# A feed-forward on TensorE: gate and up from seven products of halves, and a down stage of its own for every 512 tokens

## Chip, cores and metric

The kernel runs on one core of a Trainium2 chip. The metric is the device time of one execution in microseconds (us). Three timed runs of the kernel before lie between 2853.63 and 2855.86 us, median 2854.32.

## What is computed

One decoder layer over 2048 tokens of width 1024, in float32. The first part (an input projection, two mixers over groups of heads, an output projection and the residual) is not touched by the change. The second part is

```python
n = rms_norm(h, rms2_g[l])
h = h + (jax.nn.silu(n @ ffn_gate[l]) * (n @ ffn_up[l])) @ ffn_down[l]
return rms_norm(h, final_g)
```

with `ffn_gate` and `ffn_up` of 1024 x 2816 and `ffn_down` of 2816 x 1024, that is 22 tiles of 128 hidden channels. In the kernel, n has the channels on the partitions, so that `n @ W` is a sum over 8 slices of 128 channels.

Float32 products are made of three TensorE matmuls. Each operand is split into a high part (a cast to fp32r, on ScalarE) and a low part (the rest, a subtraction on VectorE or GpSimd), and high x high, high x low and low x high are summed in PSUM. The code has names that end in `h` and `l` for them.

## The kernel before

**First part.** The instructions are written out in an order that a planner class, `Order`, sets: `streams` lists generators (projection, mixers, output projection and so on), and the planner takes the next piece from the one that is earliest by its own account. A string that a generator yields is an event it waits for. Two generators at the end of the list prepare the second part: `ffn_w` loads the first gate and up weights, and `prep_b` prepares n for the first 1024 tokens while the last jobs of the output projection run. A job is one block of rows of the output projection; `om` events mark that its operands are ready, `op` is its PSUM tile, and its result goes to `hs` in DRAM, by way of the tile `hx`.

**Preparing n.** `prep2` (L966) loads 512 rows of `hs` for two channel slices into `hk`, scales the rows by the reciprocal norm (L977 on ScalarE, L979 on VectorE), transposes them with TensorE into the PSUM tile `tcn` (L985), and ScalarE (L995) and VectorE (L997) write the two parts into SBUF.

**Feed-forward.** `phase_b` runs over two halves of 1024 tokens. For each half all eight row tiles of h, 128x1024 each, stay in SBUF. The loop goes over 11 pairs of channel tiles. `split` loads a weight tile (512 KB) and splits it. `up(f, nb)` makes gate (`gps`) and up (`ups`) for one channel tile and 512 tokens: 8 slices x 3 matmuls for each, L1486 to L1488; then ScalarE takes silu (L1490), VectorE multiplies (L1491), and the result is split into `hh` and `hl`, which stay in SBUF. `down(nb)` multiplies the hidden block with the down weights: for each row tile and each 512 columns 2 channel tiles x 3 matmuls go into a PSUM tile `dn` (L1508 to L1510), which VectorE adds to h (L1511). After the last pair, each row tile is squared and summed on ScalarE (L1513), `row_rs` computes the reciprocal norm in nine small VectorE operations, two VectorE operations scale the row tile (L1520), and it is written out. n for the second half of the tokens is prepared inside the last pair of the first.

The order within this part is that of a scheduler in the framework. SyncE issues all loads and stores, in one queue. Tiles of a tag share a fixed number of buffers; `bt` deals out the tags that `SEQ` lists, in turn, and these are buffers that the first part has used.

Of the kernel before, what the change touches and what calls it, by code (L numbers as in the profile page):

```python
# [11 lines left out]
F32 = mybir.dt.float32  # L12
# [257 lines left out]
class K:  # L270
# [61 lines left out]
    def phase_a(self, ctx):  # L332
# [8 lines left out]
        self.n2, self.nb_ = {}, {}  # L341
# [93 lines left out]
                
# [386 lines left out]
    def out_w(self, nb):  # L822
# [3 lines left out]
        for x in range(3):  # L826
# [18 lines left out]
            for k in range(KT):  # L845
                if not k % 2:
                    if x < 2:
                        yield f"ok{k // 2}" if x else f"zk{b}.{k // 2}"
                        pair = [self.s.tile([128, 2, BLK], F32R, name="wo", tag=t, bufs=4) for t in ("nh", "nl")]
                    else:  # L850
                        pair = [self.bt("W2", "wo", [128, 2, BLK], F32R) for _ in range(2)]
                self.wo[x, k] = h, _ = [t[:, k % 2] for t in pair]
# [80 lines left out]
    def prep_b(self, nb):  # L933

        for n in range(2):
            yield f"rs{n}"
            yield f"b{nb * HP - 1}"
            yield f"a{nb * HP - 1}"
            for kp in range(KT // 2):
                if n:  # L940
                    yield f"wo2.{KT - 1}"
                    if kp == KT // 2 - 1:
                        yield f"mt{len(self.jobs(nb)) - 1}"
                yield from self.prep2(0, n, kp)

    def ffn_w(self, nb):

        nc = self.nc
        x = [j[2] for j in self.jobs(nb)]
        yield f"om{len(x) - 1 - x[::-1].index(1)}"  # L950
        yield f"b{nb * HP - 1}"
        yield f"a{nb * HP - 1}"
        yield f"gm{2 * nb - 1}"
        self.first = []
        for n in ("wg", "wu"):
            raw = self.bt("raw", "raw", [128, 1024])
            nc.sync.dma_start(out=raw, in_=self.I[n][0])
            yield
            hi, lo = [self.bt("W", n + c, [128, 1024], F32R) for c in "hl"]
            nc.scalar.copy(out=hi, in_=raw)  # L960
            yield
            nc.vector.tensor_tensor(out=lo, in0=raw, in1=hi.bitcast(F32), op=ALU.subtract)
            self.first.append((hi, lo))
            yield

    def prep2(self, half, n, kp):  # L966

        nc = self.nc
        r0 = half * 1024 + n * 512
        hb = self.hs[r0:r0 + 512, :].rearrange("(j p) d -> p j d", p=128)  # L970
        x = self.bt("raw", "hk", [128, 4, 256])
        nc.sync.dma_start(out=x, in_=hb[:, :, kp * 256:(kp + 1) * 256])
        yield
        for j in range(4):
            r = self.rsb[:, r0 // 128 + j:r0 // 128 + j + 1]
            if j % 2:
                nc.scalar.activation(out=x[:, j, :], in_=x[:, j, :], func=AF.Copy, scale=r)  # L977
            else:
                nc.vector.tensor_scalar(out=x[:, j, :], in0=x[:, j, :], scalar1=r, scalar2=None, op0=ALU.mult)  # L979
        yield 1000.0  # L980
        for i in range(2):
            k = kp * 2 + i
            ps = self.ma("tcn", [128, 512])
            for j in range(4):
                nc.tensor.transpose(out=ps[:, j * 128:(j + 1) * 128], in_=x[:, j, i * 128:(i + 1) * 128],  # L985
                                    identity=self.ident)
            yield
            if n * KT + k < 1:
                hl = self.bt("n4", "n2", [128, 2, 512], F32R)
                h, l = hl[:, 0], hl[:, 1]  # L990
            else:
                h = self.bt("n2", "n2h", [128, 512], F32R)
                l = self.bt("n2", "n2l", [128, 512], F32R)
            g = self.g2[:, k:k + 1]
            nc.scalar.activation(out=h, in_=ps, func=AF.Copy, scale=g)  # L995
            yield
# [618 lines left out]
```

## Time and profile before

| | |
|---|---|
| median of three timed runs | 2854.32 us |
| the profiled execution | 2848.36 us, of which the span is 2846.5 us |
| TensorE / VectorE / ScalarE / GpSimd busy | 96% / 50% / 35% / 24% |
| first part | until about 1360 us |
| feed-forward | from there to the last matmul at 2836.1 us |
| after the last matmul | 10.4 us |

Shares of busy time are means over both parts. Of the feed-forward alone the rows of the windows below tell: there GpSimd has nothing to do. Durations of single matmuls in the rows overlap, since a matmul starts before the one ahead of it has ended; the distance of their starts is what counts.

### The profile page before, as it was taken

The numbers are of one execution on the slowest core, as the hardware profiler recorded it, in microseconds if no ns is written. First come the engines' busy times: TensorE is split into PE (matmuls) and PEld (weight loads), VectorE is DVE, ScalarE is ACT, GpSimd is POOL, SyncE is SP. The second block draws the span as 40 slices with busy tenths as digits, with TensorE's granted clock in tenths as the row PEclk, the third lists the DMA queues.
The fourth block names the chain that finished last, engine by engine and source line by source line (L and its number), as shares of the span: only waits on it lengthen the run. The fifth ranks groups of instructions, "written<-read, shape, count | busy, mean of one in ns | idle before, by whom it ended". The sixth has DMA issues, their size and how long they took to land.

```text
span 2846.5 us, 38755 instructions
## 1 busy us (share of the span) xinstructions
PE 2719.6 (96%) x14856; PEld 2193.3 (77%) x14856; DVE 1423.0 (50%) x2878; ACT 1009.0 (35%) x1955; POOL 685.3 (24%) x1470
## 2 busy tenths in 40 slices
PE   5999899989999998999999999999999999999998
PEld 4777677777777777777888888888888888888886
DVE  6475766675666566565433333333373333333335
ACT  7455555664455454444211111111151111111112
POOL 3656465646555565310000000000000000000000
PEclk9999999999999999999999999999999999999999
DMA  4112221231121113456411111111161111111111
GB/s 146 56 60 75 90 67 57 71 100 57 60 75 56 57 64 92 158 195 219 148 45 55 49 45 45 45 45 50 49 228 51 48 50 52 45 45 45 45 45 60
DMA packets 123467, 216.56 MB, mean 76 GB/s; under 512 B 10641, under 2 KB 52337, under 8 KB 123281
## 3 DMA queue, kind: packets, MB, share of 16 engines
q1 hardware_dynamic: 123280, 214.08, 23.6%
q8 instruction: 117, 1.92, 0.3%
q14 instruction: 70, 0.57, 0.1%
HBM read 188.87 MB, written 25.17 MB: 75 GB/s over the span
## 4 chain that ended last, share of the span: by engine, by line
PE 54%; DMA 2%; DVE 1%; ACT 0%; issue 0%; SPq 0%; DVEq 0%; POOL 0%; ACTq 0%; POOLq 0%
PE gps L1486 6%; PE gps L1488 6%; PE ups L1488 6%; PE gps L1487 6%; PE ups L1486 6%; PE ups L1487 6%; PE dn L1509 6%; PE dn L1508 6%; PE dn L1510 6%; DMA hk<-hs 1%; DMA hx<-in_x 1%; PE op L901 1%; PE op L902 1%; PE op L903 1%; PE tcn L985 0%
## 5 line engine op out<-in xcount | busy, mean ns | idle before, releaser
L631 PE MATMUL zd<-nh,w_hi 128*128 128x512 f32 x832 | 358.3, 431 | 1.1 <-ACT w_hi L606 0.7
L633 PE MATMUL zd<-nh,w_lo 128*128 128x512 f32 x832 | 332.3, 399 | 6.6 <-POOL w_lo L608 6.6
L1511 DVE TENSOR_TENSOR h<-dn,h 128x512 f32<-128x512 f32 x352 | 242.7, 690 | 180.8 <-PE dn L1510 180.5
L632 PE MATMUL zd<-nl,w_hi 128*128 128x512 f32 x832 | 330.3, 397 | 0.1
L608 POOL TENSOR_TENSOR w_lo<-w_raw,w_hi 128x512 fp32r<-128x512 f32 x208 | 276.9, 1335 | 207.1 <-ACT w_hi L606 170.4
L1509 PE MATMUL dn<-wdl,hh 128*128 128x512 f32 x704 | 278.4, 395 | 0.0
L1508 PE MATMUL dn<-wdh,hh 128*128 128x512 f32 x704 | 277.7, 395 | 0.0
L1510 PE MATMUL dn<-wdh,hl 128*128 128x512 f32 x704 | 277.1, 394 | 0.0
L1488 PE MATMUL gps<-n2h,wgl 128*128 128x512 f32 x660 | 259.9, 394 | 0.0
L1488 PE MATMUL ups<-n2h,wul 128*128 128x512 f32 x660 | 259.9, 394 | 0.0
L1486 PE MATMUL gps<-n2h,wgh 128*128 128x512 f32 x660 | 259.8, 394 | 0.0
L1486 PE MATMUL ups<-n2h,wuh 128*128 128x512 f32 x660 | 259.7, 394 | 0.0
L1487 PE MATMUL gps<-n2l,wgh 128*128 128x512 f32 x660 | 259.6, 393 | 0.0
L1487 PE MATMUL ups<-n2l,wuh 128*128 128x512 f32 x660 | 259.5, 393 | 0.0
L1491 DVE TENSOR_TENSOR sgu<-sgu,ups 128x512 f32<-128x512 f32 x88 | 60.2, 684 | 396.9 <-PE ups L1488 385.8
L1453 ACT CAST wdh<-raw 128x1024 fp32r<-128x1024 f32 x44 | 46.2, 1050 | 466.0 <-PE dn L1510 250.3
L633 PEld LDWEIGHTS zd<-nh,w_lo 128*128 128x128 f32 x832 | 158.8, 191 | 46.2 <-POOL w_lo L608 9.7
L631 PEld LDWEIGHTS zd<-nh,w_hi 128*128 128x128 f32 x832 | 160.0, 192 | 32.2 <-issue 5.5
L1177 POOL TENSOR_TENSOR lm<-lm,lt 128x60 f32<-128x60 f32 (+24 forms) x496 | 171.5, 346 | 38.8
L632 PEld LDWEIGHTS zd<-nl,w_hi 128*128 128x128 f32 x832 | 160.4, 193 | 25.6 <-issue 0.7
L1490 ACT ACTIVATE sgu<-gps 128x512 f32<-128x512 f32 x88 | 52.7, 599 | 341.4 <-PE gps L1488 341.4
L1175 POOL TENSOR_TENSOR lt<-lm,ln 128x60 f32<-128x60 f32 (+24 forms) x496 | 159.4, 321 | 51.6 <-DVE ln L1159 27.3
(273 smaller groups left out, 5008.8 us busy)
## 6 DMA issues: line engine op xcount, KB each, us to landing
w_raw<-in_win SPq DMA_DIRECT2D x208, 256.0 KB, 2.6
raw<-in_wg SPq DMA_DIRECT2D x44, 512.0 KB, 4.3
raw<-in_wu SPq DMA_DIRECT2D x44, 512.0 KB, 3.6
raw<-in_wd SPq DMA_DIRECT2D x44, 512.0 KB, 3.6
mraw<-mix SPq DMA_DIRECT2D x64, 256.0 KB, 3.6
xk<-in_x SPq DMA_DIRECT2D x32, 256.0 KB, 3.7
hx<-in_x SPq DMA_DIRECT2D x32, 256.0 KB, 4.3
hs<-hx SPq DMA_DIRECT2D x32, 256.0 KB, 2.4
```

What stands on the lines that cost most here:

```text
L608: nc.gpsimd.tensor_tensor(out=wlo[:, ks, :], in0=raw, in1=whi[:, ks, :].bitcast(F32), op=ALU.subtract)
L631: nc.tensor.matmul(out=ps, lhsT=whi[:, k, :], rhs=nh, start=(k == 0), stop=False)
L632: nc.tensor.matmul(out=ps, lhsT=whi[:, k, :], rhs=nl, start=False, stop=False)
L633: nc.tensor.matmul(out=ps, lhsT=wlo[:, k, :], rhs=nh, start=False, stop=(k == KT - 1))
L1177: nc.gpsimd.tensor_tensor(out=lm[:, 0:j, i0:], in0=lm[:, 0:j, i0:], in1=lt[:, 0:j, i0:], op=ALU.add)
L1486: nc.tensor.matmul(out=ps, lhsT=w[0][:, ks], rhs=h, start=(k == 0), stop=False)
L1487: nc.tensor.matmul(out=ps, lhsT=w[0][:, ks], rhs=l, start=False, stop=False)
L1488: nc.tensor.matmul(out=ps, lhsT=w[1][:, ks], rhs=h, start=False, stop=(k == KT - 1))
L1508: nc.tensor.matmul(out=ps, lhsT=hh[:, ts], rhs=wd[f][0][:, ds], start=(f == 0), stop=False)
L1509: nc.tensor.matmul(out=ps, lhsT=hh[:, ts], rhs=wd[f][1][:, ds], start=False, stop=False)
L1510: nc.tensor.matmul(out=ps, lhsT=hl[:, ts], rhs=wd[f][0][:, ds], start=False, stop=(f == 1))
L1511: nc.vector.tensor_tensor(out=H[t][:, ds], in0=ps, in1=H[t][:, ds], op=ALU.add)
```

## The change

Gate and up. Both share the operand n. Written in blocks of halves, with the channels of n in two halves (i) and the 1024 tokens in two halves of 512 (j), the two outputs (gate, up) by two token halves are a 2 x 2 product of blocks. Before, it was eight block products; now it is seven. The operands are combinations: for the weights S1 to S4, made on GpSimd from the raw gate and up tiles, and for n the combinations X11, X21, X22, T1, T2, T3 and T4, made once for a half of the tokens in `combos` (GpSimd makes the four differences). Each operand is split as before (`wsplit`, `xsplit`); one product is 4 slices x 3 matmuls in one PSUM tile. VectorE adds and subtracts the products, and the hidden block goes to DRAM (`hid`).

Down. It is a stage of its own after gate and up of a half, once for each 512 tokens. The eight PSUM banks hold 4 row tiles x 512 columns x 2, and sum over all 22 channel tiles; the hidden block is reloaded (`hr`) and split, and the down weights are loaded once for each 512 tokens (they were loaded once for each 1024). h is loaded at the end of a stage, in tiles of 128x512 with seven buffers, added, squared, scaled and stored.

Preparing n. For the first half of the tokens it is spread over the last jobs of the output projection (`prep_b`). For the second half the combinations are made in gate and up of the first half, at the channel tiles 3, 7, 11 and 15, stored in DRAM (`xd`), and reloaded (`xl`) and split during the down stages of the first half.

The core of the diff:

```diff
-                def up(f, nb):
-                    for w, ps in ((wg[f], gps), (wu[f], ups)):
-                        for k in range(KT):
...
+            s1 = comb(u1, u2, ALU.add)
+            s2 = comb(s1, g1, ALU.subtract)
+            s3 = comb(g1, u1, ALU.subtract)
+            s4 = comb(g2, s2, ALU.subtract)
+            def prod(x):
+                w = self.wf.pop(0)
+                ps = self.bt("P8", "up", [128, 512])
+                for k in range(KT // 2):
+                    ks = slice(k * 128, (k + 1) * 128)
+                    h, l = self.n2[x, k]
+                    nc.tensor.matmul(out=ps, lhsT=w[:, 0, ks], rhs=h, start=(k == 0), stop=False)
+                    nc.tensor.matmul(out=ps, lhsT=w[:, 0, ks], rhs=l, start=False, stop=False)
+                    nc.tensor.matmul(out=ps, lhsT=w[:, 1, ks], rhs=h, start=False, stop=(k == KT // 2 - 1))
+                return ps
...
+            nc.scalar.copy(out=a, in_=prod("X11"))
+            add(b, prod("X21"), a)
+            nc.scalar.activation(out=b, in_=b, func=AF.Silu)
+            split(s2, "ws", nc.gpsimd)
+            add(a, prod("T2"), a)
+            split(s3, "ws", nc.gpsimd)
+            c = ct()
+            add(c, prod("T3"), a)
+            split(s1, "ws", nc.gpsimd)
+            p5 = prod("T1")
+            add(a, p5, a)
+            d = ct()
+            add(d, p5, c)
+            split(s4, "ws", nc.gpsimd)
+            add(a, prod("X22"), a)
+            nc.scalar.activation(out=a, in_=a, func=AF.Silu)
+            add(a, a, d, ALU.mult)
+            nc.sync.dma_start(out=self.hid[half, 1][f], in_=a)
+            split(u2, "wu")
+            add(c, prod("T4"), c)
+            add(c, b, c, ALU.mult)
+            nc.sync.dma_start(out=self.hid[half, 0][f], in_=c)
...
+    def down(self, half, n):
+        P = [self.bt("P8", "dn", [128, 512]) for _ in range(8)]
+        for f in range(NF):
+            raw = self.bt("raw", "raw", [128, D])
+            nc.sync.dma_start(out=raw, in_=I["wd"][f * 128:(f + 1) * 128, :])
+            hr = self.bt("xr", "hr", [128, 512])
+            nc.sync.dma_start(out=hr, in_=self.hid[half, n][f])
...
+                    nc.tensor.matmul(out=ps, lhsT=hh[:, ts], rhs=wh[:, ds], start=(f == 0), stop=False)
+                    nc.tensor.matmul(out=ps, lhsT=hh[:, ts], rhs=wl[:, ds], start=False, stop=False)
+                    nc.tensor.matmul(out=ps, lhsT=hl[:, ts], rhs=wh[:, ds], start=False, stop=(f == NF - 1))
...
+                h = self.bt("h", "h", [128, 512])
+                nc.sync.dma_start(out=h, in_=self.hs[rt, ds])
+                nc.vector.tensor_tensor(out=h, in0=P[2 * t + d], in1=h, op=ALU.add)
...
+        "xr": [("w_raw", 2)],
+        "S": [("xb", 4)],
+        "h": [("xb", 4)] * 4 + [("tz", 3)] * 3,
```

Three places where the order of instructions changes. The first is TensorE's row at the hand-over from the output projection. Before, it ends with the last transposes of n (`tcn`) among the matmuls of the last job (`op`):

```order
L903 MATMUL op_14243<-wo_13481,ml_14200 128x512
L985 MATMUL tcn_14272<-ident_93,hk_14238 128x128 x4
L901 MATMUL op_14243<-wo_13481,mh_14199 128x512
L902 MATMUL op_14243<-wo_13482,mh_14199 128x512
L903 MATMUL op_14243<-wo_13481,ml_14200 128x512
L985 MATMUL tcn_14288<-ident_93,hk_14238 128x128 x4
L1486 MATMUL ups_14328<-n2_13547,wuh_14120 128x512
```

Now, some 30 matmuls after the last job, with partial products (`up`) of the first channel tile, it comes to the transposes of the last quarter of the combinations:

```order
L1537 MATMUL up_14464<-n2_14338,ws_14461 128x512
L999 MATMUL tcn_14348<-ident_93,hk_14345 128x128 x4
L999 MATMUL tcn_14364<-ident_93,hk_14358 128x128 x4
L1535 MATMUL up_14446<-n2_14371,wg_13580 128x512
L1536 MATMUL up_14446<-n2_14371,wg_13580 128x512
L1537 MATMUL up_14446<-n2_14371,wg_13580 128x512
L999 MATMUL tcn_14377<-ident_93,hk_14374 128x128 x4
L1535 MATMUL up_14574<-n2_13527,wg_14558 128x512
```

All transposes of that quarter stood before the end of the output projection and stand behind it now; `hk` has two buffers.

The second place is TensorE's row in gate and up of the first half, where n of the second half is transposed. Before, in the last pair of channel tiles:

```order
L985 MATMUL tcn_18746<-ident_93,hk_18740 128x128 x4
L985 MATMUL tcn_18755<-ident_93,hk_18740 128x128 x4
L1508 MATMUL dn_18837<-wdh_18375,hh_18440 128x512
L1509 MATMUL dn_18837<-wdl_18376,hh_18440 128x512
L1510 MATMUL dn_18837<-wdh_18375,hl_18441 128x512
L1508 MATMUL dn_18847<-wdh_18375,hh_18440 128x512
L1508 MATMUL dn_18837<-wdh_18381,hh_18736 128x512
L985 MATMUL tcn_18770<-ident_93,hk_18764 128x128 x4
```

Now, at one of four channel tiles; between the rows shown and the last one stand the other matmuls of the product X11, 13 in all:

```order
L999 MATMUL tcn_16858<-ident_93,hk_16855 128x128 x4
L999 MATMUL tcn_16872<-ident_93,hk_16866 128x128 x4
L1535 MATMUL up_16932<-n2_13527,wg_16916 128x512
...
L1537 MATMUL up_16932<-n2_14355,wg_16916 128x512
L1535 MATMUL up_16946<-n2_13592,wg_16919 128x512
L999 MATMUL tcn_16883<-ident_93,hk_16880 128x128 x4
```

The load of `hk_16880` goes into the buffer that the transposes of `hk_16855` free.

The third place is the end of a down stage, on SyncE and VectorE. Before, at the end of the first half, SyncE has h tiles of the next half between the output transfers:

```order
L1525 DMA out_0<-h_14311 128x1024
L1525 DMA out_0<-h_14313 128x1024
L1473 DMA h_18981<-hs_73 128x1024
L1525 DMA out_0<-h_14315 128x1024
L1525 DMA out_0<-h_14317 128x1024
L1473 DMA h_18983<-hs_73 128x1024
```

Now, at the end of the first down stage, the eighth h tile of the same stage (`h_18767`) is loaded behind the outputs of the first two row tiles:

```order
L1622 DMA out_0<-h_18681 128x512
L1622 DMA out_0<-h_18686 128x512
L1622 DMA out_0<-h_18708 128x512
L1622 DMA out_0<-h_18713 128x512
L1612 DMA h_18767<-hs_73 128x512
L1622 DMA out_0<-h_18735 128x512
```

and VectorE adds the eighth bank (`dn_17773`) to it behind the scaling of the first three row tiles:

```order
L1620 SCALAR_TENSOR_TENSOR h_18708<-h_18708,rn_y_18721,gbf_17764 128x512
L1620 SCALAR_TENSOR_TENSOR h_18713<-h_18713,rn_y_18721,gbf_17764 128x512
L320 SCALAR_TENSOR_TENSOR rn_y_18748<-rn_t_18749,rn_y_18748 128x1
L319 SCALAR_TENSOR_TENSOR rn_t_18749<-rn_x_18745,rn_y_18748 128x1
L320 SCALAR_TENSOR_TENSOR rn_y_18748<-rn_t_18749,rn_y_18748 128x1
L319 SCALAR_TENSOR_TENSOR rn_t_18749<-rn_x_18745,rn_y_18748 128x1
L320 SCALAR_TENSOR_TENSOR rn_y_18748<-rn_t_18749,rn_y_18748 128x1
L1620 SCALAR_TENSOR_TENSOR h_18735<-h_18735,rn_y_18748,gbf_17764 128x512
L1620 SCALAR_TENSOR_TENSOR h_18740<-h_18740,rn_y_18748,gbf_17764 128x512
L1613 TENSOR_TENSOR h_18767<-dn_17773,h_18767 128x512
```

Before, an h tile was loaded a whole half ahead of its last addition; now one tile of each down stage is loaded after outputs of that stage.

## Rows read from the trace of the kernel before

**Rows 1.** Head of the page: span, then busy us (share) of each engine.

```profile
span 2846.5 us, 38755 instructions
...
PE 2719.6 (96%) x14856; PEld 2193.3 (77%) x14856; DVE 1423.0 (50%) x2878; ACT 1009.0 (35%) x1955; POOL 685.3 (24%) x1470
```

**Rows 2.** The chain that ended last: share of the span by engine.

```profile
PE 54%; DMA 2%; DVE 1%; ACT 0%; issue 0%; SPq 0%; DVEq 0%; POOL 0%; ACTq 0%; POOLq 0%
```

**Rows 3.** Waits of PE from 1250 us on: us in total, times, longest.

```profile
PE tcn L985 <- DVE hk L979: 7.7, 6, 2.5
PE gps L1486 <- DVE n2l L997: 0.4, 1, 0.4
```

**Rows 4.** Stretches: length, busy PE PEld DVE ACT POOL, PEclk, DMA share, GB/s.

```profile
1300.00:1350.00 50.00, 45.81 (x203) 35.98 (x203) 24.89 (x50) 23.46 (x47) 0.00 (x0) 0.97 0.70 236
1350.00:1400.00 50.00, 49.62 (x219) 40.06 (x218) 19.84 (x36) 17.05 (x26) 0.00 (x0) 1.00 0.54 195
...
1500.00:2000.00 500.00, 500.00 (x2160) 405.37 (x2159) 169.84 (x219) 81.29 (x106) 0.00 (x0) 1.00 0.15 47
...
2120.00:2836.00 716.00, 716.00 (x3092) 580.16 (x3090) 261.89 (x387) 123.21 (x175) 0.00 (x0) 1.00 0.16 49
```

**Rows 5.** Costliest groups: busy us, mean ns, idle before.

```profile
L1511 DVE TENSOR_TENSOR h<-dn,h 128x512 f32<-128x512 f32 x352 | 242.7, 690 | 180.8 <-PE dn L1510 180.5
...
L608 POOL TENSOR_TENSOR w_lo<-w_raw,w_hi 128x512 fp32r<-128x512 f32 x208 | 276.9, 1335 | 207.1 <-ACT w_hi L606 170.4
```

**Rows 6.** Groups of ScalarE (feed-forward; L536 whole span) and VectorE (feed-forward).

```profile
L1494 ACT CAST hh<-sgu 128x512 fp32r<-128x512 f32 x84 | 52.1, 620 | 264.5 <-DVE sgu L1491 264.5
L1453 ACT CAST wdh<-raw 128x1024 fp32r<-128x1024 f32 x41 | 43.1, 1051 | 461.5 <-PE dn L1510 250.3 <-PE dn L1509 129.9 <-PE ups L1488 75.1
...
L536 ACT ACTIVATE xk<-xk,rn_y 128x128 f32<-128x128 f32 x64 | 20.2, 392 | 5.8 <-DMA w_raw<-in_win 2.8 <-DVE rn_y L301 2.7 <-DMA xk<-in_x 0.3
...
L1454 DVE TENSOR_TENSOR wdl<-raw,wdh 128x1024 fp32r<-128x1024 f32 x42 | 51.1, 1217 | 6.7 <-ACT wdh L1453 6.6
...
L1520 DVE SCALAR_TENSOR_TENSOR h<-h,rn_y,gbf 128x512 f32<-128x512 f32 x26 | 18.4, 748 | 0.1
...
L319 DVE SCALAR_TENSOR_TENSOR rn_t<-rn_x,rn_y 128x1 f32<-128x1 f32 x41 | 8.3, 215 | 0.3
L320 DVE SCALAR_TENSOR_TENSOR rn_y<-rn_t,rn_y 128x1 f32<-128x1 f32 x40 | 6.0, 154 | 0.2
```

**Rows 7.** Single lines, ns min/median/max: two of the first part, L1495 of the feed-forward.

```profile
L608 POOL TENSOR_TENSOR w_lo<-w_raw,w_hi x188: 1259/1286/2407, 102.3 to 1097.5; 128x512 fp32r<-128x512 f32 x188
...
L1065 DVE TENSOR_TENSOR bk<-bh,pinv x15: 650/701/1832, 112.1 to 1086.3; 128x512 f32<-128x512 f32 x15
...
L1495 DVE TENSOR_TENSOR hl<-sgu,hh x84: 681/693/694, 1439.9 to 2826.2; 128x512 fp32r<-128x512 f32 x84
```

**Rows 8.** Short stretches at the hand-over to the feed-forward, columns as in rows 4.

```profile
1343.00:1346.00 3.00, 1.50 (x6) 1.29 (x7) 2.10 (x5) 1.96 (x6) 0.00 (x0) 0.81 0.94 330
1346.00:1350.00 4.00, 4.00 (x16) 3.15 (x16) 0.70 (x2) 1.87 (x4) 0.00 (x0) 0.71 0.77 262
...
1355.00:1360.00 5.00, 5.00 (x27) 4.16 (x26) 1.88 (x4) 3.73 (x7) 0.00 (x0) 1.00 1.03 351
```

**Rows 9.** PE from 1344 us: start, us, instruction, idle before it.

```profile
1344.49 0.98 PE L985 MATMUL tcn<-ident,hk 128*128 128x128 f32 x4 [2.03 <-DVE hk L979]
...
1346.13 0.63 PE L903 MATMUL op<-wo,ml 128*128 128x512 f32 x1
1346.55 0.63 PE L901 MATMUL op<-wo,mh 128*128 128x512 f32 x1
```

**Rows 10.** A DMA issue of the page: KB, us to landing.

```profile
hx<-in_x SPq DMA_DIRECT2D x32, 256.0 KB, 4.3
```

**Rows 11.** The last matmul and the last scaling: start, us.

```profile
2835.68 0.40 PE L1510 MATMUL dn<-wdh,hl 128*128 128x512 f32 x1
...
2842.00 1.41 DVE L1520 SCALAR_TENSOR_TENSOR h<-h,rn_y,gbf 128x512 f32<-128x512 f32 x2
```

More of the change, by code (lines that the diff above doesn't have):

```diff
@@ L850, in out_w @@
                     else:
-                        pair = [self.bt("W2", "wo", [128, 2, BLK], F32R) for _ in range(2)]
-                self.wo[x, k] = h, _ = [t[:, k % 2] for t in pair]
+                        pair = [self.bt("W2", "wo", [128, 2, BLK], F32R) for _ in range(1 if k == KT - 2 else 2)]
+                        if k == KT - 2:
+                            pair.append([self.s.tile([128, BLK], F32R, name="wo", tag="k", bufs=2) for _ in range(2)])
+                self.wo[x, k] = h, _ = [t[k % 2] if isinstance(t, list) else t[:, k % 2] for t in pair]
                 nc.scalar.copy(out=h, in_=raws[k])
@@ L933, in prep_b @@
     def prep_b(self, nb):
[L935 to L944, printed above, removed]
+        n = len(self.jobs(nb))
+        x = [j[2] for j in self.jobs(nb)]
+        yield "rs0"
@@ L946, in ffn_w @@
+        yield f"b{nb * HP - 1}"
+        yield f"a{nb * HP - 1}"
+        yield f"gh{2 * nb - 1}.1"
+        for k in range(KT // 2):
+            if k == 2:
+                yield f"om{n - 1 - x[::-1].index(1)}"
+            for c, t in self.combos(0, k, "rs1"):
+                if t is None:
+                    yield c
+                    continue
+                if k == KT // 2 - 1 and c == "T1":
+                    yield f"om{n - 1}"
+                yield from self.xsplit(c, k, t)
     def ffn_w(self, nb):
@@ L948, in ffn_w @@
         nc = self.nc
-        x = [j[2] for j in self.jobs(nb)]
-        yield f"om{len(x) - 1 - x[::-1].index(1)}"
+        yield "rs0"
         yield f"b{nb * HP - 1}"
         yield f"a{nb * HP - 1}"
[L953 to L964, printed above, removed]
@@ L966, in prep2 @@
-    def prep2(self, half, n, kp):
-        nc = self.nc
[L969 to L972, printed above, removed]
-        yield
[L974 to L996, printed above, removed]
-            nc.vector.scalar_tensor_tensor(out=l, in0=ps, scalar=g, in1=h.bitcast(F32),
-                                           op0=ALU.mult, op1=ALU.subtract)
-            self.n2[n, k] = (h, l)
-            yield
@@ new lines, in xsplit, with wsplit @@
+    def xsplit(self, c, k, src):
+        nc = self.nc
+        if k < 2:
+            h, l = [self.bt("n2", "n2", [128, 512], F32R) for _ in range(2)]
+        else:
+            hl = self.bt("n4", "n2", [128, 2, 512], F32R)
+            h, l = hl[:, 0], hl[:, 1]
+        nc.scalar.copy(out=h, in_=src)
+        yield
+        nc.vector.tensor_tensor(out=l, in0=src, in1=h.bitcast(F32), op=ALU.subtract)
+        self.n2[c, k] = h, l
+        yield
+    def wsplit(self, src, name, eng):
+        nc = self.nc
+        hl = self.bt("W", name, [128, 2, 512], F32R)
+        nc.scalar.copy(out=hl[:, 0], in_=src)
+        yield
+        eng.tensor_tensor(out=hl[:, 1], in0=src, in1=hl[:, 0].bitcast(F32), op=ALU.subtract)
+        self.wf.append(hl)
+        yield
@@ new lines, in phase_b @@
+        self.hid = {(h, n): self.dram.tile([NF, 128, 512], F32, name=f"hid{h}_{n}")
+                    for h in range(T // 1024) for n in range(2)}
+        self.xd = self.dram.tile([KT // 2, 7, 128, 512], F32, name="xd")
+        self.gbf = None
+        for half in range(T // 1024):
+            more = (half + 1) * 1024 < T
+            self.up(half, more)
+            self.load = iter([(k, i) for k in range(KT // 2) for i in range(7)]) if more else iter([])
+            for n in range(2):
+                self.down(half, n)
+            for _ in self.load:
+                raise AssertionError
```

227 lines of the change are left out of this document (125 added, 102 removed).

## The prediction

> **What bounds the kernel now.** I read the head of the page first, then the chain that ended last, then the waits of TensorE, then the stages. The span is 2846.5 us and TensorE is busy for 96% of it [rows 1]; the chain is 54% TensorE matmuls, with DMA at 2% and VectorE at 1% [rows 2]. From 1250 us to the end TensorE waits for only two things: 7.7 us in six waits for scaled rows of the second norm, and 0.4 us once [rows 3]. All of these lie where the out projection hands over to the feed-forward. From there TensorE has no gap: 500.00 us of work in 500 us from 1500 on, and 716.00 in 716 later [rows 4]. In that stage VectorE is busy for 170 us of 500, ScalarE for 81, GpSimd for nothing, and the DMA engines stand at a share of 0.15. So the feed-forward is worth its number of matmuls and nothing else, as long as the four helpers keep up. One matmul costs 500 / 2160 = 0.2315 us there [rows 4].
>
> **Removed: 528 matmuls.** Before, one channel tile of one half of the tokens took 2 matrices x 2 blocks of 512 tokens x 8 slices x 3 = 96 matmuls for gate and up. Now it takes 7 products x 4 slices x 3 = 84. Over 22 tiles and 2 halves that is 44 x 12 = 528 fewer, or 528 x 0.2315 = 122.2 us. The down matmuls stay at 2112 and the transposes at the same number. The 352 additions of VectorE into h, of 690 ns each [rows 5], become 32; they were hidden under TensorE, so they give back nothing.
>
> **Added beside TensorE, while gate and up run.** One channel tile is now 84 x 0.2315 = 19.4 us of TensorE. GpSimd gets 4 combinations and 4 low halves, 8 x 1.335 = 10.7 us [rows 5]. ScalarE gets 7 casts at 0.62 [rows 6] and a copy and two silus of the same size, 6.2 us. VectorE gets 3 low halves and 9 additions or products, 12 x 0.69 = 8.3 us [rows 5, 7]. All are under 19.4, and each weight half is cast as soon as the product six before it is done, five products or 13.9 us ahead of its use. I cost this at nothing; it would cost the excess over 19.4 on whichever engine ran over.
>
> GpSimd idled in this stage and now works beside VectorE. The rows of the first stage show that the two get in each other's way: a VectorE product with both inputs in SBUF takes 701 ns in the middle but up to 1832 beside a busy GpSimd, and the low half of the feed-forward, with GpSimd idle, never over 694; a GpSimd low half goes from 1259 to 2407 [rows 7]. The Trainium skill, "SBUF — State Buffer", section "SBUF: two separate sides", says that a VectorE instruction with two SBUF inputs and a GpSimd instruction exclude one another for their whole length; the trace agrees, since 1832 is about one of each. By that rule five VectorE instructions per tile (three low halves, two products) wait at most one GpSimd instruction each. From the rows the worst is then 8.3 + 5 x 1.335 = 15.0 us on VectorE and 8 x 2.407 = 19.3 us on GpSimd, both still under 19.4. So nothing by either reading, but GpSimd's end of it is narrow, and it is a rival below.
>
> **Added in down.** One tile is 24 matmuls, 5.6 us. ScalarE casts 512 and 1024 columns (0.62 + 1.05), VectorE splits them (0.69 + 1.22) [rows 6, 7]; in the first down stage each gets two more of 0.62 and 0.69 per tile. The most is 3.3 us on VectorE. The weights and the hidden block are 768 KB per tile, 142 GB/s, and with two reloaded combinations 1.3 MB, 236 GB/s. The trace shows 351 GB/s and 330 GB/s in short stretches [rows 4, 8]. Zero, therefore; were the 236 GB/s of the stretch from 1300 on all there is, it would still just fit. The other end is the 195 GB/s of the next stretch [rows 4]: 14 tiles with two reloads would take 6.7 us instead of 5.6, +16.
>
> **The seams are where something is lost**, and each is priced apart. E is the end of TensorE's work in the stage.
>
> Out projection to gate and up: +4 us. Before, this seam lost 7.7 us in waits [rows 3], and a wait of 2.03 us is followed by matmuls 0.43 us apart instead of 0.2315, at a granted clock of 0.81 and 0.71 [rows 8, 9]: some 1.6 us more. Now the last quarter of the combinations comes after the last projection matmul: load (4.3 us, the nearest row is hx [rows 10]), four scalings at 0.39 on ScalarE [rows 6], transposes, an evacuation the size of a cast, four GpSimd differences of 1.335, cast and split of 1.3. With only two load buffers the four loads go in pairs, and the last pieces are there at about E+20. Partial products of the first two channel tiles fill 70 matmuls, 16.2 us, and the transposes 1.8. A few us stay open, and the earlier quarters wait as those of before did. Bounds: -9 (all waits of before gone) to +20 (two such chains bare).
>
> Combinations for the second half of the tokens, made within gate and up of the first: 4 x 2 = +8 us. The third transpose group needs a buffer that the first group frees; 13 matmuls stand between (3.0 us), and the load alone is 4.3 [rows 10] with a VectorE scaling of some 0.7 behind it. The stall is about 2 us, near the longest of before's six, 2.5 [rows 3]. Bounds 0 to 16.
>
> First to second block of a half in down: 2 x 6 = +12 us. Seven h buffers serve eight tiles. The eighth load is queued on SyncE behind four output transfers, and the last of these waits for VectorE's final scaling of the second row tile. VectorE begins its additions 21 matmuls (4.9 us) before E and has through that scaling 7 additions (4.8), some 22 small operations at 0.15 to 0.22 (3.9), a low half of 0.69, two of 1.22 and four scalings of 0.75 [rows 5 to 7], together 14.8: E+10. With 0.5 to issue, 4.3 to land [rows 10] and 0.69 to add, bank 8 is free at E+15.5. TensorE has 7 banks x 2 tiles x 3 = 42 matmuls, 9.7 us. The rest is 5.8 us. Bounds 0 to 10 each.
>
> Down to the gate and up of the second half: +6 us. GpSimd's first combinations need the buffers that h holds until its output has landed (about E+7), then two combinations and a low half; the first products cover part. Bounds 0 to 14. Gate and up to down: +1, all loads stand ahead.
>
> End: +9 us. Now 10.4 us pass from the last matmul to the end of the span [rows 11]. The eighth load sits there as above, without the next stage's splits: issue at E+7.3, landed at E+11.6, then addition (0.69), square (a cast and a small operation, 0.8), nine small operations (1.6) and two scalings (1.5), and the 3.1 us that follow the last scaling now: E+19.3. Bounds +3 to +12.
>
> Clock: after waits of 4 to 6 us I count 1.6 us for each of three, +5. Bounds 0 to 12.
>
> **The sum.** -122.2 + 4 + 8 + 12 + 6 + 1 + 9 + 5 = -77. The profiled execution took 2848.4 us (span 2846.5 and 1.9 around it), so 2771. The runs shown have a median of 2854.3, 5.9 above it, so I forecast 2777.
>
> **Rivals.**
> 1. The seams are covered by filler work and transfers are quicker than the rows taken: only the tail and a few us remain, 2854 - 122 + 12 = 2744. For it: TensorE did not wait once in before's hand-over between the halves. Against it: seven buffers for eight tiles is a hard order. 0.15.
> 2. The seams cost their upper bounds: 20 + 16 + 20 + 14 + 12 + 12 = 94 instead of 45, so 2826. For it: 256 KB transfers share the queue with large loads, and VectorE is in order. Against it: most bounds stack independent accidents. 0.13.
> 3. Slower than before: GpSimd becomes the bound of gate and up. Its eight operations per tile are in one in-order queue with VectorE's five two-input operations against it; from 19.4 / 8 = 2.4 us each the stage stretches, and from (19.4 + 77 / 44) / 8 = 2.65 us the whole gain is gone. At 3 us it would be 24 us per tile, 44 x 4.6 = +202, and 2978. Against it: the mean in the first stage, beside a busier VectorE, is 1.335, and only the longest of 188 reaches 2.41. 0.05.
> 4. The change does not do what it says, since each half product also waits for a chain of casts across three engines and TensorE idles once per product: at 0.25 us for each of 308 products, the gain shrinks by 77 to 2854, no change. Against it: a lead of five products. 0.05.
>
> **How the numbers follow.** Forecast 0.62, its own range 2755 to 2800; rivals 0.15, 0.13, 0.05, 0.05. A measurement here tells about 0.2% (6 us) from no change. Faster: forecast, rivals 1 and 2, 0.90, and a part of rival 4, 0.91; same 0.03; slower 0.06. The range from 2740 to 2826 leaves out rivals 3 and 4 and the edges of 1.
>
> **What would show it.** Matmuls per channel tile of gate and up still 0.2315 apart, and 3696 of them; GpSimd near 1.3 us and half busy in that stage. Waits of TensorE at three kinds of places only: transposes of scaled rows, the eighth bank at a block's end, and the first low halves of the second half. The last output about 19 us after the last matmul. It is wrong if TensorE waits for casts or low halves in the middle of gate and up, if loads in the first down stage take twice their time, or if the waits at the seams add to under 15 or over 90 us.

## The result and the profile after

The changed kernel takes 2789.88 us (median of 4 runs, 2788.56 to 2792.0) against 2853.98 us (4 runs, 2849.23 to 2855.86): a ratio of 0.9779, 95% interval 0.9762 to 0.9796. The forecast was 2777, its range 2740 to 2826. The profiled execution took 2790.3 us, 19 above the sum of the prediction in its own terms (2771).

First the stages: length, busy time of PE, PEld, DVE, ACT, POOL, granted clock, DMA share, GB/s.

```profile
1375.00:1411.00 36.00, 24.96 (x87) 17.38 (x88) 22.61 (x33) 16.78 (x32) 16.11 (x12) 0.76 0.25 78
1420.00:1500.00 80.00, 79.09 (x351) 64.04 (x350) 38.09 (x52) 29.07 (x52) 53.30 (x39) 1.00 0.35 116
1500.00:1832.00 332.00, 329.68 (x1447) 267.10 (x1446) 160.36 (x212) 118.41 (x203) 189.79 (x137) 1.00 0.35 114
1832.00:1966.00 134.00, 133.91 (x574) 107.37 (x572) 70.88 (x112) 53.76 (x82) 0.00 (x0) 1.00 0.63 199
2100.00:2500.00 400.00, 400.00 (x1728) 324.78 (x1727) 192.75 (x262) 126.90 (x210) 235.07 (x169) 1.00 0.26 89
2525.00:2653.00 128.00, 127.92 (x549) 102.56 (x547) 52.98 (x84) 39.37 (x58) 0.00 (x0) 1.00 0.47 148
```

Gate and up of the second half (the row from 2100) look like the feed-forward of before [rows 4]: TensorE without a gap, 400 / 1728 = 0.2315 us for a matmul, although GpSimd now works 59% of the time. In the first down stage (from 1832) the DMA engines move 199 GB/s and TensorE does not wait for them. What is lost in waits stands at the seams, the hand-overs from one stage to the next, but for 3.2 us at transposes within gate and up of the first half. The waits of TensorE from 1200 us on, as total, times and longest:

```profile
PE tcn L999 <- DVE hk L994: 14.4, 11, 2.9
PE dn L1594 <- DVE h L1613: 9.1, 2, 4.6
PE tcn L999 <- ACT hk L992: 6.9, 5, 2.2
PE up L1536 <- DVE n L1023: 6.0, 2, 5.0
PE up L1535 <- ACT n L1021: 1.8, 2, 1.4
...
PE up L1537 <- POOL ws L1033: 1.7, 2, 1.2
PE up L1535 <- ACT ws L1031: 1.6, 1, 1.6
...
```

Where the kernel before had 8 us of waits [rows 3] there are now 41 (the rows left out, 2.3 us, lie in the first part), most of them of the kinds that were forecast: transposes of scaled rows, the eighth bank, the first weights of the second half. One kind was not: 7.8 us for the two parts of a combination (`n`) at the hand-over from the output projection, 6.0 of it for low halves. The two places with the longest waits of all, start, us, instruction and idle time before it:

```profile
1385.56 0.80 PE L1536 MATMUL up<-n,ws 128*128 128x512 f32 x1 [5.00 <-DVE n L1023]
1390.46 1.09 PE L999 MATMUL tcn<-ident,hk 128*128 128x128 f32 x4 [1.54 <-DVE hk L994]
...
1396.06 0.80 PE L1535 MATMUL up<-n,wg 128*128 128x512 f32 x1 [1.43 <-ACT n L1021]
1396.78 0.80 PE L1536 MATMUL up<-n,wg 128*128 128x512 f32 x1
1397.38 0.63 PE L1537 MATMUL up<-n,wg 128*128 128x512 f32 x1
1397.81 1.05 PE L999 MATMUL tcn<-ident,hk 128*128 128x128 f32 x4
...
1970.35 0.50 PE L1594 MATMUL dn<-wd,hh 128*128 128x512 f32 x1 [4.43 <-DVE h L1613]
```

The first rows are that hand-over, "the seam" from here on. After the wait of 5.00 us the matmuls stand some 0.43 to 0.7 us apart until 1401, at 1.2 GHz: the granted clock of that stretch is 0.76, and 17.1 us of it are at half. The last row is the wait for the eighth bank, between the two blocks of 512 tokens; the same wait in the second half is 4.63 us. In both cases VectorE stood before the eighth addition until the h tile landed, and this tile was issued behind four output transfers (VectorE's row, then SyncE's):

```profile
1969.60 0.69 DVE L1613 TENSOR_TENSOR h<-dn,h 128x512 f32<-128x512 f32 x1 [3.34 <-DMA h<-hs]
```

```profile
1961.23 2.97 SPq L1622 DMA_DIRECT2D out<-h  x4
1966.05 0.33 SPq L1612 DMA_DIRECT2D h<-hs  x1
```

The four outputs were issued by 1964.2, and SyncE then waited another 1.8 us, here until the first of them had landed (1966.03), since the eighth tile takes the buffer of the first; its waits from 1960 to 1968 us show it:

```profile
SPq L1612 <- DMA out<-h: 1.8, 1, 1.8
```

The last matmul starts at 2772.19, and the span ends at 2788.5, 15.9 us after that matmul's end (10.4 in the kernel before).

Why TensorE waited 5.00 us at 1385 stands in VectorE's row:

```profile
1376.59 0.81 DVE L928 TENSOR_TENSOR ssb<-ssb 128x4 f32<-128x4 f32 x1 [1.25 <-ACT osq L922]
1377.43 1.22 DVE L929 TENSOR_SCALAR ssb<-ssb 128x4 f32<-128x4 f32 x1
1378.69 0.17 DVE L296 TENSOR_SCALAR rsb<-ssb 128x4 int32<-128x4 int32 x1
1378.89 1.14 DVE L299 TENSOR_TENSOR ssb<-rsb 128x4 f32<-128x4 f32 x1
1380.06 1.19 DVE L300 SCALAR_TENSOR_TENSOR ssb<-ssb 128x4 f32<-128x4 f32 x1
1381.29 0.16 DVE L301 SCALAR_TENSOR_TENSOR rsb<-ssb,rsb 128x4 f32<-128x4 f32 x1
...
1382.55 2.96 DVE L1023 TENSOR_TENSOR n<-xf,n 128x512 fp32r<-128x512 f32 x3
```

Twelve small operations make the reciprocal norm of the last 512 tokens, which nothing needs before the second half. They stand ahead of the low halves `n`, and four of them take 0.8 to 1.2 us while GpSimd works; L299 and L300 take 0.16 a little later. GpSimd's row:

```profile
1376.09 1.29 POOL L1006 TENSOR_TENSOR xf<-xf 128x512 f32<-128x512 f32 x1 [0.86 <-ACT xf L1002]
1377.34 1.29 POOL L1523 TENSOR_TENSOR S<-raw 128x512 f32<-128x512 f32 x1
1378.70 1.30 POOL L1523 TENSOR_TENSOR S<-S,raw 128x512 f32<-128x512 f32 x1
1379.96 1.27 POOL L1523 TENSOR_TENSOR S<-raw 128x512 f32<-128x512 f32 x1
```

### The profile page after: what moved, and what is told of

It is laid out like the page before. It is cut to its first block, busy times and chain, and to the rows that moved or that the text cites. A ratio compares the mean times of both kernels' runs of the same rounds, so it can differ in the third digit from the quotient of the medians.

```text
span 2788.5 us, 40062 instructions
## 1 busy us (share of the span) xinstructions
PE 2621.8 (94%) x14328; PEld 2104.8 (75%) x14328; DVE 1537.4 (55%) x2962; ACT 1214.9 (44%) x2351; POOL 1223.1 (44%) x1854
## 4 chain that ended last, share of the span: by engine, by line
PE 53%; DVE 4%; DMA 3%; ACT 2%; POOL 2%; issue 1%; SPq 0%; DVEq 0%; ACTq 0%; POOLq 0%
PE up L1537 10%; PE up L1536 10%; PE up L1535 10%; PE dn L1596 5%; PE dn L1594 5%; PE dn L1595 5%; DMA hk<-hs 2%; PE op L902 1%; PE op L903 1%; PE op L904 1%; POOL lm L1212 1%; POOL lt L1210 1%; PE zd L630 1%; PE zd L632 1%; PE zd L631 0%
## 5 line engine op out<-in xcount | busy, mean ns | idle before, releaser
L1541 DVE TENSOR_TENSOR C<-up,C 128x512 f32<-128x512 f32 x308 | 208.5, 690 | 300.3 <-PE up L1537 299.0
L1033 POOL TENSOR_TENSOR ws<-S,ws 128x512 fp32r<-128x512 f32 x176 | 248.8, 1415 | 280.8 <-ACT ws L1031 271.1
L1594 PE MATMUL dn<-wd,hh 128*128 128x512 f32 x704 | 278.8, 396 | 9.1 <-DVE h L1613 9.1
L1536 PE MATMUL up<-n,ws 128*128 128x512 f32 x704 | 278.9, 396 | 6.0 <-DVE n L1023 6.0
L1537 PE MATMUL up<-n,ws 128*128 128x512 f32 x704 | 279.7, 397 | 1.7 <-POOL ws L1033 1.7
L1535 PE MATMUL up<-n,ws 128*128 128x512 f32 x704 | 278.6, 396 | 1.9 <-ACT ws L1031 1.6
L1596 PE MATMUL dn<-wd,hh 128*128 128x512 f32 x704 | 280.2, 398 | 0.0
L1595 PE MATMUL dn<-wd,hh 128*128 128x512 f32 x704 | 279.0, 396 | 0.0
L1523 POOL TENSOR_TENSOR S<-raw 128x512 f32<-128x512 f32 x88 | 128.9, 1464 | 296.2 <-DMA out<-h 274.5
L1031 ACT CAST ws<-S 128x512 fp32r<-128x512 f32 x176 | 108.8, 621 | 316.8 <-PE up L1537 304.3
L1587 DVE TENSOR_TENSOR hh<-hr,hh 128x512 fp32r<-128x512 f32 x88 | 62.4, 710 | 249.9 <-ACT hh L1585 249.9
L1585 ACT CAST hh<-hr 128x512 fp32r<-128x512 f32 x88 | 54.4, 620 | 300.9 <-PE dn L1595 296.3
L630 PEld LDWEIGHTS zd<-nh,w_hi 128*128 128x128 f32 x832 | 160.9, 193 | 31.5 <-issue 4.8
L1594 PEld LDWEIGHTS dn<-wd,hh 128*128 128x128 f32 x704 | 132.8, 189 | 42.1 <-DVE h L1613 9.9
```

Of the source, the lines that this page charges most:

```text
L630: nc.tensor.matmul(out=ps, lhsT=whi[:, k, :], rhs=nh, start=(k == 0), stop=False)
L1033: eng.tensor_tensor(out=hl[:, 1], in0=src, in1=hl[:, 0].bitcast(F32), op=ALU.subtract)
L1535: nc.tensor.matmul(out=ps, lhsT=w[:, 0, ks], rhs=h, start=(k == 0), stop=False)
L1536: nc.tensor.matmul(out=ps, lhsT=w[:, 0, ks], rhs=l, start=False, stop=False)
L1537: nc.tensor.matmul(out=ps, lhsT=w[:, 1, ks], rhs=h, start=False, stop=(k == KT // 2 - 1))
L1541: nc.vector.tensor_tensor(out=o, in0=ps, in1=b, op=op)
```

## Experiments

For the seam I compare one stretch in each profile: from the first matmul of the output projection ("the projection" below) to the first matmul of the last product (T4) of the first channel tile. It is 290.9 us in the changed kernel. Before, from the first projection matmul to the end of the projection, it was 244.1 (1115.4 to 1359.5); with the 76 matmuls of gate and up that now lie in it, 76 x 0.2315 = 17.6, it would be 261.7. So the seam costs 29.2 us. The stretch is used because whole times scatter: the first projection matmul starts anywhere between 1112.7 and 1123.9 us in the profiles of this study, though most of them run the same instructions up to there; the time spent at half clock before it differs (67 us in the profile of before, 77 in that of after). The same scatter reaches into the beginning of the stretch: its first microseconds are at half clock for 4.2 us before and for 11.3 in the changed kernel, so that some 3.5 of the 29.2 us belong to the execution and not to the seam. Differences of 2 or 3 us between stretches are read with this beside them. The median of the kernel before itself lies between 2853.98 and 2859.43 us in the rounds of this study.

**An eighth product.** The product T4 is run twice.

```diff
+                for k in range(KT // 2 if x == "T4" else 0):
...
+                    nc.tensor.matmul(out=ps, lhsT=w[:, 0, ks], rhs=h, start=False, stop=False)
...
```

> The product T4 is computed twice into its PSUM tile, so each channel tile has 96 matmuls again, as before the change; the hidden block of half of the tokens is wrong by that. If TensorE alone bounds gate and up, the 528 extra matmuls cost 528 x 0.2315 = 122 us: about 2912, and what is above the 2854 of before, some 58 us, is what the rest of the change costs. Rival: a cast or GpSimd chain sets part of the pace of a channel tile; then the extra matmuls fill its gaps and the time rises by clearly less, under 100 us.

2912.65 us in one run, 122.8 above the changed kernel. The profile shows where: from T4 of the first tile to the first down matmul it takes 482.3 us instead of 421.6, and gate and up of the second half 496.2 instead of 434.4, together 122.5 more. So gate and up are TensorE's alone, the seven products give 122 us as forecast, and the rest of the change costs about 2912.65 - 2853.98 = 59 us.

**GpSimd twice.** Every GpSimd operation of gate and up is issued twice.

```diff
-        eng.tensor_tensor(out=hl[:, 1], in0=src, in1=hl[:, 0].bitcast(F32), op=ALU.subtract)
+        for _ in range(2 if eng is nc.gpsimd else 1):
+            eng.tensor_tensor(out=hl[:, 1], in0=src, in1=hl[:, 0].bitcast(F32), op=ALU.subtract)
...
+                nc.gpsimd.tensor_tensor(out=t, in0=a, in1=b, op=op)
                 nc.gpsimd.tensor_tensor(out=t, in0=a, in1=b, op=op)
```

> Each of the eight GpSimd operations of a channel tile in gate and up is issued twice (same result). From the trace one costs 1.42 to 1.46 us, so GpSimd would need 23.0 us for a tile against 19.4 us of matmuls. If it is hidden now, only the excess shows, 3.6 us for each of 44 tiles: about +160, 2950, and TensorE waits for low halves of GpSimd. Rival: GpSimd is on the path already, through the chain comb, cast, low half; then most of its extra 11.5 us shows for each tile: over +350, 3140 or more.

2990.05 us in one run, +200. The two largest waits of TensorE from 1420 us on:

```profile
PE up L1539 <- POOL ws L1034: 129.2, 67, 5.2
PE dn L1596 <- DVE h L1615: 8.5, 2, 4.3
```

GpSimd is hidden in the changed kernel: of some 500 us added (44 tiles x 11.5 as expected), less than half shows. The expected 160 us came out as 131 us more idle time of TensorE in gate and up. The rest goes with the clock: 123 us of gate and up were at half clock, against 7 in the changed kernel, which is worth up to 58 us, since the matmuls between the waits are slower too.

**Late norm.** The reciprocal norm of the last 512 tokens is taken out of the end of the projection.

```diff
-                self.newton(s1, self.rsb[:, bs], s2)
+                if x < 2:
+                    self.newton(s1, self.rsb[:, bs], s2)
+                else:
+                    self.late = (s1, self.rsb[:, bs], s2)
...
+            if f == 1 and more:
+                self.newton(*self.late)
```

> The reciprocal norm of the last 512 tokens (11 small VectorE operations, needed only for the second half of the tokens) is moved from the end of the output projection to the second channel tile of gate and up. In the trace these operations stand on VectorE from 1376.6 to 1382.6 us, ahead of four low halves that are ready, and TensorE waits 5.00 us for one of them. Theory: that order is the cause of this wait, and of part of the 17 us at half clock behind it: 4 to 9 us faster, 2781 to 2786. Rival: the loads of the last quarter, two buffers for four loads, end last anyway; then TensorE waits the same time at the transposes instead, and the time stays at 2788 to 2792.

2787.36 us (2780.48 to 2791.37), ratio to the kernel before 0.9752 (0.9729 to 0.9775): not to be told from the changed kernel by time. The edit moves ten of the twelve operations. The stretch is 286.3, 4.6 shorter, and the wait of 5.00 is gone (the longest of that kind is 1.0). The scheduler moved the operations back to where they were, but between the low halves instead of ahead of them. The clock did not follow: 17.1 us at half as before, behind five waits of 0.5 to 1.9 us. So VectorE's order caused that wait. What it is worth can't be read from this stretch alone: it begins with 6.8 us at half clock instead of 11.3, which alone makes 2.2 of the 4.6 us.

**Eight h buffers.** The buffer of the squares becomes the eighth h tile.

```diff
-        "h": [("xb", 4)] * 4 + [("tz", 3)] * 3,
-        "sq": [("dg", 1)],
+        "h": [("xb", 4)] * 4 + [("tz", 3)] * 3 + [("dg", 1)],
+        "sq": [("k", 2)],
```

> An eighth h buffer (the one that took the squares, which go to the two buffers of the reloaded combinations instead). Theory: the eighth h load, behind four output transfers, holds the eighth PSUM bank; then both waits of 4.4 and 4.6 us go, with some us at half clock behind them, and the 15.9 us after the last matmul shrink by 3 or more: 10 to 16 us faster, 2774 to 2780. Rival: VectorE's own queue holds the bank (additions, small operations and scalings ahead of the eighth addition); then the waits shrink by less than 1 us each: 2786 to 2790.

2771.46 us (2765.12 to 2776.43), ratio 0.9698 (0.9674 to 0.9721), clear of the changed kernel's. The waits from 1250 us on no longer hold a row for `dn`:

```profile
PE tcn L999 <- DVE hk L994: 12.4, 10, 2.6
PE tcn L999 <- ACT hk L992: 6.3, 6, 2.0
PE up L1536 <- DVE n L1023: 6.0, 2, 5.0
PE up L1537 <- POOL ws L1033: 4.1, 2, 2.5
```

The last matmul (at 2756.65) ends 12.6 us ahead of the end of the span (2769.7), not 15.9. The eight additions of a block now follow each other without a gap. So 9 us at the two block ends and 3.3 at the end were the eighth load; VectorE's queue alone did not hold the bank. Half clock at the two block ends, 3.4 us each, is gone too. The seam is as it was (291.1). Some of the 18 us in all lies before the projection (its first matmul starts 3.9 us earlier in this profile).

**Two more load buffers.** The last two row loads of the last quarter get buffers of their own.

```diff
+                if second and k == KT // 2 - 1 and n:
+                    x = self.s.tile([128, 4, 128], F32, name="hk", tag="k", bufs=2)
+                else:
+                    x = self.bt("xr", "hk", [128, 4, 128])
```

> The last two of the four row loads of the last quarter of the combinations get two buffers of their own (free after the last projection matmul), so they need not wait for the transposes of the first two. In the trace they are issued at about 1391.6 us, behind those transposes. Theory: the loads in pairs end the seam; issued by 1380, they bring the last transposes 8 us or more forward, and the time falls by 6 to 12 us, to 2778 to 2784. Rival: VectorE's order (the late reciprocal norm, then the low halves) and GpSimd's four differences end last; then TensorE waits for these instead, and at most 3 us are gained.

2789.35 us (2784.71 to 2791.41), ratio 0.976 (0.9742 to 0.9779); the stretch is 291.0. SyncE's row shows that the four loads are issued together, 12 us earlier for the last two:

```profile
1375.95 3.10 SPq L991 DMA_DIRECT2D hk<-hs  x4
```

Yet nothing is gained. My theory fell: in the changed kernel TensorE reached the second pair of transposes (1397.81, in the rows of the first section) without waiting. They came late because of what stood ahead of them.

**All three.** The late norm, the eight h buffers and the two more load buffers, as in the diffs above.

> Eight h buffers, the late reciprocal norm and the two more load buffers together. If the three places are independent, their gains add: 18 + 5 + 8 us below 2790, about 2758 (2752 to 2764). Rival: the two edits of the seam lift the same wait, and only the larger shows: 2764 to 2771.

2770.63 us (2767.17 to 2773.47), ratio 0.97 (0.9682 to 0.9717), as the eight buffers alone. The stretch is 288.5, 2.5 below that with the two load buffers alone, but it begins with 5.8 us at half clock instead of 11.2, which makes 2.7. The gains of the seam's two edits are too small to show in the time.

**Differences on VectorE.** Beside the three edits, all differences of the first half's combinations move from GpSimd to VectorE.

```diff
-        sub = lambda o, a, b: nc.gpsimd.tensor_tensor(out=X[o], in0=X[a], in1=X[b], op=ALU.subtract)
+        eng = nc.vector if second else nc.gpsimd
+        sub = lambda o, a, b: eng.tensor_tensor(out=X[o], in0=X[a], in1=X[b], op=ALU.subtract)
```

> As the three edits, and the 16 differences of the first half's combinations run on VectorE instead of GpSimd. In the trace one takes 1.29 to 1.73 us on GpSimd, in a chain of four at the end of the seam, and about 0.69 on VectorE. Theory: that chain ends the seam once the loads are early; 2 to 4 us faster than the three edits. Rival: VectorE is in order and has all low halves of the seam too; what GpSimd gives back, its queue takes, and the time is that of the three edits within 2 us.

2779.52 us (2775.43 to 2784.14), ratio 0.9732 (0.9712 to 0.9752): slower than the three edits by some 9 us. The stretch is 291.1, with 23.9 us at half clock in the seam instead of 10.2 and with 69 matmuls of gate and up in it instead of 75; the next one up to the first down matmul is 7.5 us longer (429.1 instead of 421.6). Neither theory held. Up to 1440 us TensorE waits 7.5 us for casts of combinations, 3.3 with the three edits. The last of these casts starts 297.7 us after the first projection matmul instead of 286.1. That a VectorE with both the low halves and the differences in one queue delivers later than the two engines side by side fits this; it was not tried apart from the clock.

**Eight buffers and late norm.** The two diffs above, without the load buffers.

> Eight h buffers and the late reciprocal norm, without the two more load buffers. Theory: the late norm takes 4 to 5 us out of the seam whatever else is there (its wait of 5.00 us goes), so this is 4 to 5 us below the eight h buffers alone in the stretch from the first projection matmul to the last product of the first tile (290.9 us before the edit, 286 after), and 2765 to 2769 in all. Rival: the seam is an in-order chain whose end does not move; then the stretch stays within 2 us of 290.9 and the time at 2770 to 2773.

2772.79 us (2763.25 to 2781.66), ratio 0.971 (0.9682 to 0.9737). The stretch is 287.5, 3.4 to 3.6 below that without the late norm, with as much half clock at its beginning (11.4 us); the time does not resolve it. Counted from the end of the projection, which leaves that beginning out, the last cast of a combination starts after 31.2 to 32.3 us in the late norm, the three edits and this run, and after 34.0 to 35.2 in the changed kernel, the eighth product, the eight buffers and the load buffers. So the late norm is worth some 3 us of the seam.

**Later transposes.** As the last one, and:

```diff
-                yield 1000.0, None
+                yield 3000.0 if k < 2 else 1000.0, None
```

> As the two edits, and the planner puts the transposes of the first two quarters 2 us later in TensorE's order (its own allowance of 1000 ns between load and transpose becomes 3000). In the trace TensorE waits 18 us at the transposes of scaled rows, most of it before the last projection matmul. Theory: these waits stand there because the order has the transposes too early for loads of 4.1 us; later ones cost little, the waits fall to under 10 us, and the stretch from first projection matmul to last product of the first tile falls by 5 us or more below that of the two edits. Rival: more of the third quarter slips behind the last projection matmul, the chain there grows by as much, and the stretch is no shorter.

2779.4 us (2770.59 to 2784.42), ratio 0.9734 (0.9708 to 0.976); the stretch is 293.2, longer. The waits at the transposes fell from 18 to 11 us, but others came:

```profile
PE tcn L1002 <- ACT hk L995: 6.4, 5, 1.7
PE up L1540 <- ACT n L1024: 4.8, 5, 1.4
PE tcn L1002 <- DVE hk L997: 4.7, 5, 2.7
PE up L1542 <- POOL ws L1036: 3.1, 1, 3.1
PE op L902 <- DVE hx L920: 2.4, 1, 2.4
```

That is the rival: 36 of the 64 transposes are ahead of the last projection matmul, 44 without this edit, and what slips behind it is paid there. The time is not clear of that of the last one.

**Three quarters, and two.** The last quarter of the combinations is left out, then the last two.

```diff
         for k in range(KT // 2):
+            if k >= 3:
+                for c in self.XN:
+                    self.n2[c, k] = self.n2[c, 3 - 1]
+                continue
```

> The last quarter of the combinations of the first half is left out: its loads, transposes, differences and splits; gate and up of the first half use the third quarter in its place, so the result is wrong by that. Only the stretch from the first projection matmul to the last product of the first tile is compared: 290.9 us now, and 261.7 if it were as long as before the change plus the 76 matmuls of gate and up in it. Theory: the last quarter, whose operands have no place until the last projection matmul, is nearly all of the loss: 262 to 270. Rival: each quarter costs about the same, by waits at its transposes: 281 to 285.

> The last two quarters are left out in the same way (the second stands in for them). Theory: nothing is left to gain over leaving out the last alone but some waits of the third at its transposes: 258 to 265. Rival (each costs the same): 273 to 278.

With three quarters the stretch is 276.4 us (72 matmuls of gate and up in it), with two 261.5. Without a loss they would be 259.0 and 257.2 (244.1 + 72 x 0.2315, less 1.8 us of transposes for each quarter left out). So the loss is 29.2 us with four quarters, 17.4 with three, 4.3 with two: the last costs 12, the third 13, the first two 4 together. The beginning at half clock (11.3, 5.9 and 11.3 us, 4.2 before) is in these numbers; with half of each difference taken off they are 26, 17 and 1, so 9 for the last and 16 for the third. I had expected the last alone or all alike; it is the last two. With three quarters a long wait is still there, for a cast (waits from 1250 to 1440 us):

```profile
PE tcn L1003 <- DVE hk L998: 7.9, 5, 2.4
PE up L1539 <- ACT n L1025: 5.3, 1, 5.3
PE tcn L1003 <- ACT hk L996: 4.4, 5, 1.3
```

What sets the third and the last quarter apart from the first two is in the code of the change: their split operands go into the buffers that hold the projection's weights and its `mh` and `ml` (class `n4`). The third quarter begins when four jobs of the projection are left, and the splits of the last quarter's differences after the last job (`om` events in `prep_b`). That this is the reason is read from the code and was not tried by other buffers.

## Why the prediction was right, and which term was mis-sized

Each term of the sum, in us, beside what the profiles and runs gave:

| term | forecast | measured |
|---|---|---|
| 528 matmuls | -122.2 | -122.5 (eighth product, the two stages in the profile) |
| before the projection | 0 | +4.8 (1115.4 to 1120.2, half clock of the execution) |
| out projection to gate and up | +4 | +29.2 |
| combinations of the second half | +8 | +3.2 (four waits, longest 0.9) |
| blocks in down | +12 | +9.1 |
| down to gate and up | +6 | +3.3 |
| gate and up to down | +1 | 0 |
| end | +9 | +5.5 |
| clock | +5 | about +6 behind the three later waits (13.7 us at half, 1.5 of it idle); the seam's part is in its own term |
| down's matmuls | 0 | +4 |
| sum | -77 | -57, and -58 between the two spans |

The mechanism held. Gate and up are bound by TensorE, the seven products give their matmuls in full, and the helpers hide: no wait in 400 us of the second half. Rival 3 had its point of decision at 2.65 us for a GpSimd operation; from 2100 to 2500 us their groups take 1.31 to 1.47 on average. A chain of waits once per product (rival 4) does not exist. GpSimd and VectorE do get in each other's way there: VectorE's products with both inputs in SBUF take 1.20 us in the middle (2100 to 2500 us), its additions with one input in PSUM 0.69. It cost TensorE nothing in gate and up; it cost at the seam, where small operations stretched. This is the contention that the Trainium skill names ("SBUF — State Buffer", "SBUF: two separate sides"). In down no transfer is late: with 1.3 MB for a tile (1836 to 1892 us) the DMA engines moved 251 GB/s, and TensorE was busy for all 56 us.

The step of the forecast that failed is the term "Out projection to gate and up: +4 us", whose bounds ended at +20. It had the last pieces ready at E+20; they were split at E+35 (the cast at 1408, with E at 1373). Three things made it longer. The wait for VectorE's order (5.0, of which some 3 came back with the late norm) was not seen: I followed the chain of the combinations and not what else stood in VectorE's queue. The third quarter was counted as hidden but for waits like those of before, and the run without the last shows that it costs at least as much; some 9 of the 29 us lie ahead of E, where the projection takes 252.6 us instead of 243.8. And the clock: 17 us at half behind the wait, where one short stretch of 3.4 us had been priced. Over the stretch TensorE's idle time is 31.5 us against 13.3 before, and it spends about 14 us more at half clock, 21 with the beginning that the first part leaves behind; half of 21 and the 18 make some 26 of the 29, as a few us of idle time lie inside the half clock. The split of the loss between the waits and the clock is worked out from these rows, not tried.

The load pairs, which that step named as the reason, were not it: with four buffers nothing changed. Every other seam was over-priced, by 1 to 5 us and 15 in all, which hides more than half of the 25 us missing at this one; with the first part, down's matmuls and the clock the forecast is still 20 short. That it is not further off is luck.

The eighth bank was right as a mechanism and in its order (eighth load behind four outputs), and its size, 5.8 forecast and 4.4 and 4.6 measured, was near. Two errors in it cancel: VectorE's second scaling ended some 2 us earlier than the forecast had it (1963.85, 7.7 us after E), and SyncE's wait of 1.8 us for the buffer was not in it. Of the losses tried it is the only one that could be taken back: eight h buffers, 2771.46 us, ratio 0.9698 to the kernel before, beats both kernels, and no other version is measurably faster. The late norm on top of it does not show in the time.

Down's matmuls are 134 / 574 = 0.2334 and 128 / 549 = 0.2332 us apart, against 0.2315 in gate and up, some 4 us over 2112 of them; the prediction took one distance for all. In the first down stage the extra stands mostly where the three matmuls of one PSUM bank end and those of the next begin (0.2353 there, 0.2320 and 0.2326 between the three). Why is open.

## What to carry to other kernels

Where one engine has no gap, a saving in its instructions comes in full, and the cost of the rewrite stands where one stage hands over to the next: price there every instruction that is queued on the waiting engine, not only those of the chain. An operand that needs space still held by the previous stage can't be prepared ahead; more load buffers gave nothing back here. A ring that is one buffer short of a stage's tiles is worth a look first: here one buffer gave back 9 us at two block ends and 3 at the end.

## What the runs showed of the hardware

Beside a busy GpSimd, VectorE operations of four elements per partition can take nearly as long as a GpSimd operation of 512: 0.81, 1.22, 1.14 and 1.19 us, where L299 and L300 take 0.16 without it. By the rows of the first section each of the four ended within 0.03 us of the end of the GpSimd operation beside it. One of the slow ones (L929) has a single tensor as input; in the late norm the same line, with GpSimd idle beside it, took 0.17. In a chain of short operations this adds up: the twelve took 6 us instead of some 2.

Half clock comes in runs behind waits, and a row of short waits is followed by more of it than one long wait: 17 us behind the seam's waits (5.0, 1.5, 1.7 and 1.4 us between 1380 and 1396), as much in the late norm behind waits of which none was over 1.9 us (10.2 in the two later runs with that edit), but 3.4 behind a single one of 4.4, and 123 us in gate and up where TensorE waited 67 times for GpSimd, 129 us in all.
